# Phase tables made whole in the setup, and sums of MLP weight factors made during the mixer blocks

## The chip, the cores and the metric

One core of one Trainium2 chip runs the whole program. The metric is the device time of one execution in microseconds; lower is better.

## What is computed

One layer of a hybrid encoder over 2048 positions (16 learned meta tokens are put ahead and dropped at the end), width 1024. A chunked SSD mixer (16 heads of 64, state 128, short causal convolution) and an S5 mixer (32 groups of 16 channels, 64 complex states each) run side by side on the normed input, are gated and projected; a squared-ReLU MLP of width 4096 follows. All of it is held to float32 accuracy.

```
z, xbc, dt_raw, u_s5, gates = split(rmsnorm(h) @ w_in)
y_a = ssd_branch(z, xbc, dt_raw, ...)
y_b = s5_branch(u_s5, ...)          # h_t = a * h_(t-1) + B u_t, complex, causal
h = h + (sigmoid(g_a) * y_a + sigmoid(g_b) * y_b) @ w_out
h = h + square(relu(rmsnorm(h) @ w_ff_in)) @ w_ff_out
return rmsnorm(h)[:, 16:]
```

## The kernel before

Every large product is done as three: each operand is split into a rounded high part (`fp32r`, a cast on ScalarE) and the low rest (a subtraction on VectorE or GpSimd), and `mm3` (L243 to L245) issues high x high, high x low and low x high into one PSUM bank.

**Setup.** `s5_setup` is a generator that is pumped between the products of `u` (tiles `uw`, four blocks of 512 rows). It makes the S5 constants: powers of the discrete poles, the input and output matrices (`cst`), the causal kernels (`kpad`), and a table `tab` of phases, cosine and sine of k times eight steps' angle for 16 pairs of groups. `double` lengthens such a table by multiplying what is there by its last entry: six VectorE instructions per step. The table is made to `K0` = 64 entries and stored in the DRAM tile `tabd`. The recurrence needs KA + 1 = 259 entries.

**Mixer blocks.** Four blocks of 512 rows. In each, for four head groups: the convolved products (XBC), then the gate products (ZG), with the SSD steps hung behind them; then two more gate products (GB), the GLU products and the output products (OUT). Weights come in units of 0.5 MB that are split into 1 MB (`wu`, three buffers, two units fetched ahead). In block 0 the raw unit is loaded by SP (`wst`), split by ScalarE and GpSimd and stored (`wsd`); later blocks load the split unit through GpSimd's queue. In block 0 the whole S5 recurrence runs too, one of 16 pairs every two steps: `load_w` (L519) loads the pair's constants and the first 65 entries of its table into `s5tb` and lengthens them there to 259, in three steps of four VectorE instructions (L538 to L541) with the scratch tile `s5tu`. `states` uses the table, cosine and sine, in the lines L584, L585, L593 and L594.

**MLP.** Rows in three blocks of 768, 768 and 512, each cut in two halves; both products use Winograd's form of Strassen's scheme, seven products where eight would be, so that seven weight factors per group are wanted: three pieces of the weights themselves and four sums of them. There are 8 inner rounds (`di`) with four groups each, 28 products per round, 32 groups in all. In the first row block `Weights.make` loads two raw units per group through SP, makes the four sums on GpSimd (L1366 to L1369, L1380 to L1383), and for each factor `weight` casts (ScalarE, L1341), splits (VectorE or GpSimd by the table `ENG`, L1342) and stores it (SP, L1343) in the DRAM tile `wcd`. The factor's tile `wc` has three buffers, and one factor is made ahead of the product that is running. The other two row blocks read the factors back through GpSimd's queue (L1352).

**What sets the order.** Each engine works its instructions off in order. The order is made by a scheduler from the order in which the program is written; `tc.issue_after(mm)` holds back only those instructions that stand on the engine of `mm`. Loads and stores on SP, and GpSimd's loads, stand in the order of those engines.

```
            tu = pl.tile([P, P], F32, name="s5tu", tag="s5tu")
            done = K0
            while done < KA:
                ...
                V.scalar_tensor_tensor(tb[:, 1, o_], xi, yr, tu[:, :m], op0=ALU.mult, op1=ALU.add)
```

## Time and profile before

| | us |
|---|---|
| median of 3 runs | 3317.12 (3313.74 to 3323.17) |
| the profiled execution's own time | 3315.93 |
| its span, first to last instruction | 3314.2 |

| engine | busy us | share of the span | instructions |
|---|---|---|---|
| TensorE | 3087.5 | 93% | 18353 |
| VectorE | 2119.2 | 64% | 4364 |
| ScalarE | 1227.8 | 37% | 2569 |
| GpSimd | 1417.8 | 43% | 1736 |

The profile is one execution; the times of its stages are read from stretches of it, given in us from the span's start. A row of a stretch gives each engine's busy time, the share of TensorE's clock that was granted, the mean busy share of the 16 transfer engines, and what they moved. Matmuls are pipelined, so that TensorE's busy time is an upper bound of its work. A wait is put down to the event that came last. The shares over the whole span say little, since the stages have different limits.

### The profile page before, as it was taken

The numbers are of one execution on the slowest core, as the hardware profiler recorded it, in microseconds if no ns is written. First come the engines' busy times: TensorE is split into PE (matmuls) and PEld (weight loads), VectorE is DVE, ScalarE is ACT, GpSimd is POOL, SyncE is SP. The second block draws the span as 40 slices with busy tenths as digits, with TensorE's granted clock in tenths as the row PEclk, the third lists the DMA queues.
The fourth block names the chain that finished last, engine by engine and source line by source line (L and its number), as shares of the span: only waits on it lengthen the run. The fifth ranks groups of instructions, "written<-read, shape, count | busy, mean of one in ns | idle before, by whom it ended". The sixth has DMA issues, their size and how long they took to land. (4 is left out here: it accounts for less than half of the span.)

```text
span 3314.2 us, 50076 instructions
## 1 busy us (share of the span) xinstructions
PE 3087.5 (93%) x18353; PEld 2747.0 (83%) x18353; DVE 2119.2 (64%) x4364; ACT 1227.8 (37%) x2569; POOL 1417.8 (43%) x1736
## 2 busy tenths in 40 slices
PE   7989889998999999998999889898979999989998
PEld 6678777887888778876788788888879999989998
DVE  8689999526844476426764577667675555475555
ACT  5354444434422443324433443334442121142222
POOL 3356566523522244213442465665652222243343
PEclk9999989999999999999999999999999999999999
DMA  6376665775555654565756767777788888889998
GB/s 225 117 220 172 186 168 170 280 248 185 171 197 187 220 156 168 204 229 179 226 174 210 275 254 268 261 272 267 268 292 282 248 248 247 247 286 369 360 358 279
DMA packets 299493, 776.56 MB, mean 234 GB/s; under 512 B 94736, under 2 KB 136848, under 8 KB 270448
## 3 DMA queue, kind: packets, MB, share of 16 engines
q0 software_dynamic: 88832, 411.21, 37.3%
q1 hardware_dynamic: 207808, 360.93, 33.0%
q8 instruction: 146, 2.39, 0.3%
q10 hardware_dynamic: 2608, 1.22, 0.1%
q14 instruction: 99, 0.81, 0.1%
HBM read 560.48 MB, written 214.88 MB: 234 GB/s over the span
## 5 line engine op out<-in xcount | busy, mean ns | idle before, releaser
L1501 DVE TENSOR_TENSOR acc<-acc,p 128x512 f32<-128x512 f32 x330 | 225.8, 684 | 167.0 <-PE p L245 164.8
L243 PE MATMUL pd<-hnh,wc 128*128 128x384 f32 (+1 forms) x896 | 291.2, 326 | 30.9 <-DMA wc<-wcd 20.6
L243 PE MATMUL pd<-wu,xnh 128*128 128x512 f32 x768 | 310.9, 405 | 4.0 <-DMA wu<-wsd 3.1
L245 PE MATMUL pd<-wu,xnl 128*128 128x512 f32 x768 | 310.5, 405 | 0.0
L244 PE MATMUL pd<-wu,xnh 128*128 128x512 f32 x768 | 309.5, 403 | 0.0
L245 PE MATMUL pd<-hnh,wc 128*128 128x384 f32 (+1 forms) x896 | 290.0, 327 | 14.2 <-DVE wc L1342 11.7
L244 PE MATMUL pd<-hnl,wc 128*128 128x384 f32 (+1 forms) x896 | 290.1, 324 | 0.0
L227 POOL DMA_DIRECT2D wu<-wsd x168 | 96.0, 572 | 374.2 <-PE pd L245 309.0
L243 PE MATMUL pd<-xnh,wu 128*128 128x512 f32 (+1 forms) x640 | 232.1, 363 | 9.0 <-DMA wu<-wsd 8.9
L1352 POOL DMA_DIRECT2D wr<-wcd x227 | 121.1, 534 | 273.7 <-PE pd L245 135.0
L244 PE MATMUL pd<-xnl,wu 128*128 128x512 f32 (+1 forms) x640 | 230.2, 360 | 0.0
L245 PE MATMUL pd<-xnh,wu 128*128 128x512 f32 (+1 forms) x640 | 229.9, 360 | 0.0
L1352 POOL DMA_DIRECT2D wc<-wcd x221 | 117.4, 531 | 254.5 <-PE pd L245 136.6
L243 PEld LDWEIGHTS pd<-hnh,wc 128*128 128x128 f32 x896 | 172.1, 192 | 36.4 <-ACT hnh L990 12.2
L749 DVE SCALAR_TENSOR_TENSOR cacc<-craw,conv,cacc 128x512 f32<-128x512 f32 (+1 forms) x192 | 172.1, 897 | 31.8 <-ACT cacc L746 27.1
L245 PEld LDWEIGHTS pd<-hnh,wc 128*128 128x128 f32 x896 | 172.1, 192 | 20.8 <-DVE wc L1342 15.0
L217 POOL TENSOR_TENSOR wu<-wst,wu 128x1024 fp32r<-128x1024 f32 x56 | 137.6, 2458 | 90.7 <-ACT wu L216 85.6
L243 PEld LDWEIGHTS pd<-wu,xnh 128*128 128x128 f32 x768 | 146.8, 191 | 34.9 <-DMA wu<-wsd 4.0
L245 PEld LDWEIGHTS pd<-wu,xnl 128*128 128x128 f32 x768 | 147.2, 192 | 31.6
L244 PEld LDWEIGHTS pd<-wu,xnh 128*128 128x128 f32 x768 | 147.1, 191 | 31.0 <-issue 0.2
L244 PEld LDWEIGHTS pd<-hnl,wc 128*128 128x128 f32 x896 | 172.2, 192 | 0.0
L243 PEld LDWEIGHTS pd<-xnh,wu 128*128 128x128 f32 x640 | 125.2, 196 | 26.1 <-issue 10.8
(1012 smaller groups left out, 9984.0 us busy)
## 6 DMA issues: line engine op xcount, KB each, us to landing
wu<-wsd POOLq DMA_DIRECT2D x168, 1024.0 KB, 5.2
wr<-wcd POOLq DMA_DIRECT2D x227, 512.0 KB, 5.0
wcd<-wc SPq DMA_DIRECT2D x224, 512.0 KB
wc<-wcd POOLq DMA_DIRECT2D x221, 512.0 KB, 5.5
wsd<-wu SPq DMA_DIRECT2D x56, 1024.0 KB
wst<-in_w SPq DMA_DIRECT2D x60, 512.0 KB
csb<-csd SPq DMA_DIRECT2D x16, 1024.0 KB
xt<-in_x SPq DMA_DIRECT2D x28, 512.0 KB
```

The lines of the kernel that those rows point to most:

```text
L217: eng.tensor_tensor(t[:, 1], raw, t[:, 0].bitcast(F32), op=ALU.subtract)
L227: nc.gpsimd.dma_start(t, wsd[u - U_XBC])
L243: T.matmul(ps, lh, rh, start=first, stop=False, skip_group_check=open_)
L244: T.matmul(ps, lh, rl, start=False, stop=False, skip_group_check=open_)
L245: return T.matmul(ps, ll, rh, start=False, stop=last, skip_group_check=open_).ins
L749: V.scalar_tensor_tensor(acc[:, :n], raw[:, k:k + n], conv[:, mt, k:k + 1], acc[:, :n], op0=ALU.mult, op1=ALU.add)
L1352: nc.gpsimd.dma_start(t, wcd[di * 28 + j])
L1501: V.tensor_tensor(o, o, pv, op=ALU.add)
```

## The change

**Tables.** `K0` falls from 64 to 8: the setup makes 9 entries for all 16 pairs as before. A new function `phases` copies these for a quarter of the pairs (`NT` = 4) into a tile `tg`, lengthens them with `double` to 259 entries, six steps of six VectorE instructions, and stores them in `tabd`; it is called four times, after every second of the eight pieces of the setup. `load_w` loads the finished table, and its twelve VectorE instructions per pair are gone.

**Sums.** 30 of the 32 groups of MLP weights get their four sums early: 8 groups in mixer block 0, 9 in block 1, 9 in block 2, 4 in block 3 (`EARLY`). `ff_early` loads a group's two raw units through SP (tiles `era`, `erb`, two buffers), makes each sum (on VectorE in block 0, on GpSimd in the others), and `ff_split` casts it (ScalarE), splits it (VectorE) and stores it in `wcd` (SP). `early_step` draws these steps behind the units of the GLU and OUT products (in block 3 behind GLU alone). In the first MLP row block, the factors of these groups that are sums are loaded from `wcd` through GpSimd's queue into the same three `wc` buffers; the three plain pieces are made as before, with every split on VectorE. In all, 120 factors are made in the mixer blocks instead of the first row block and read back there once more.

```diff
-K0 = 64
+K0 = 8
+NT = 4
+EARLY = (8, 9, 9, 4)
...
-        nc.sync.dma_start(tabd, tab)
...
+        def phases(q0):
+            qs = slice(q0, q0 + NT)
+            tg = pl.tile([P, NT, 2, KA + 1], F32, name="tg", tag="tg")
+            S.copy(tg[:, :, :, 0:K0 + 1], tab[:, qs])
+            xa, xb = [x.rearrange("p q m -> p (q m)").rearrange("p (q m) -> p q m", q=NT) for x in (ua, ub)]
+            done = K0
+            while done < KA:
+                m = min(done, KA - done)
+                double(tg[:, :, 0, :], tg[:, :, 1, :], xa, xb, done, m)
+                done += m
+            nc.sync.dma_start(tabd[:, qs], tg)
...
+            if i % 2 == 1:
+                phases((i // 2) * NT)
...
-            nc.sync.dma_start(tb[:, :, 0:K0 + 1], tabd[:, q])
+            nc.sync.dma_start(tb, tabd[:, q])
...
-            tu = pl.tile([P, P], F32, name="s5tu", tag="s5tu")
-            done = K0
-            while done < KA:
...
-                V.tensor_scalar(tu[:, :m], xi, yi, None, op0=ALU.mult)
-                V.scalar_tensor_tensor(tb[:, 0, o_], xr, yr, tu[:, :m], op0=ALU.mult, op1=ALU.subtract)
-                V.tensor_scalar(tu[:, :m], xr, yi, None, op0=ALU.mult)
-                V.scalar_tensor_tensor(tb[:, 1, o_], xi, yr, tu[:, :m], op0=ALU.mult, op1=ALU.add)
-                done += m
...
+    def ff_sums(g, v, room, eng):
+        a11, a12, a21, a22 = v
...
+        if g % 4 < 2:
+            s1 = tt("s1", a21, a22, ALU.add)
+            yield 4, s1
+            s2 = tt("s2", s1, a11, ALU.subtract)
+            yield 1, s2
+            yield 2, tt("s3", a11, a21, ALU.subtract)
+            yield 6, tt("s4", a12, s2, ALU.subtract)
...
+    def ff_split(t, w, eng, i):
+        S.copy(t[:, 0], w)
+        eng.tensor_tensor(t[:, 1], w, t[:, 0].bitcast(F32), op=ALU.subtract)
+        nc.sync.dma_start(wcd[i], t.rearrange("p a k n -> p (a k n)").bitcast(F32))
+
+    def ff_early(pl, groups, eng):
+        def load(g):
+            wa, wb = [pl.tile([P, D], F32, name=nm, tag="er", bufs=2) for nm in ("era", "erb")]
+            ff_load(g, wa, wb)
+            return wa, wb
+        raw = load(groups[0])
+        for n, g in enumerate(groups):
+            v, m = ff_pieces(g, *raw)
...
+            for j, w in ff_sums(g, v, room, eng):
+                t = pl.tile([P, 2, m, 512 // m], F32R, name="ew", tag="ew", bufs=2)
+                ff_split(t, w, V, g * 7 + j)
+                if j == (6 if m == 4 else 3) and n + 1 < len(groups):
+                    raw = load(groups[n + 1])
+                yield
...
+        early = ff_early(pool("early%d" % b, stack=e_st, side="right"), range(g0, g0 + EARLY[b]), G if b else V)
+        slots = 8 if b == NB - 1 else 16
...
-            rhs_group([(b, U_GLU + q * 2 + i) for i in range(2)], y5h, y5l, evac_glu)
+            rhs_group([(b, U_GLU + q * 2 + i) for i in range(2)], y5h, y5l, evac_glu, step=early_step)
...
         def make(self):
...
+            for g in range(32):
+                wa, wb = ff_raw(fw, "wa"), ff_raw(fw, "wb")
+                ff_load(g, wa, wb)
...
+                ws = {0: a11, 3: a12, 5: a22} if m == 4 else {0: a11, 2: a21, 6: a22}
+                early = g < sum(EARLY)
+                if not early:
+                    ws |= dict(ff_sums(g, v, lambda nm: ff_sum(fw, nm).rearrange("p (k n) -> p k n", k=m), G))
+                for j in range(7):
+                    if j in ws:
+                        yield self.weight(ws[j], "v" if early else ENG[g % 4][j], m, g * 7 + j)
+                        continue
+                    t = wcs[0].tile([P, D], F32R, name="wc", tag="wc", bufs=wcs[1])
+                    nc.gpsimd.dma_start(t, wcd[g * 7 + j])
+                    yield t.rearrange("p (a k n) -> p a k n", a=2, k=m)
```

The order on three engines shows it. On VectorE in mixer block 0, before the change, the steps of a pair's table (`s5tu`, `s5tb`) stand among the convolution (`cacc`) and the SSD output (`y`):

```order
L538 TENSOR_SCALAR s5tu<-s5tb 128x64
L749 SCALAR_TENSOR_TENSOR cacc<-craw,conv,cacc 128x528
L870 TENSOR_SCALAR yss<-yss 128x1
L860 TENSOR_TENSOR y__3611<-y__3611,py 128x256
L539 SCALAR_TENSOR_TENSOR s5tb<-s5tb,s5tu 128x64
L860 TENSOR_TENSOR y__3611<-y__3611,py 128x256
L540 TENSOR_SCALAR s5tu<-s5tb 128x64
L866 TENSOR_TENSOR y__3611<-y__3611,zg 128x256
L541 SCALAR_TENSOR_TENSOR s5tb<-s5tb,s5tu 128x64
```

With the change that engine's table work stands in the setup, here the step of 128 entries of one quarter, among the low parts of the normed rows (`xnl`) that the `u` products wait for:

```order
L361 TENSOR_TENSOR ua<-tg 128x512
L362 TENSOR_TENSOR ub<-tg 128x512
L279 SCALAR_TENSOR_TENSOR xnl<-ntp,wmix,xnh 128x128 x2
L363 TENSOR_TENSOR tg<-ua,ub 128x4x128
L279 SCALAR_TENSOR_TENSOR xnl<-ntp,wmix,xnh 128x128 x2
L364 TENSOR_TENSOR ua<-tg 128x512
L365 TENSOR_TENSOR ub<-tg 128x512
L279 SCALAR_TENSOR_TENSOR xnl<-ntp,wmix,xnh 128x128
L366 TENSOR_TENSOR tg<-ua,ub 128x4x128
```

The table work has left the stretch where pairs and SSD steps alternate, for the one where the normed rows are made. On SP in the last products of mixer block 0, with the change:

```order
L227 DMA wsd<-wu 128x2048
L217 DMA wst<-in_w 128x1024
L938 DMA wcd<-ew 128x1024 x2
L908 DMA era<-in_w 128x1024
L1308 DMA yt<-yd 128x512
L938 DMA wcd<-ew 128x1024
L909 DMA erb<-in_w 128x1024
L938 DMA wcd<-ew 128x1024 x2
```

Loads and stores of the early sums (`era`, `erb`, `wcd<-ew`) stand between the unit loads (`wst`) and the last load of S5 outputs (`yt`), where before `wsd` and `wst` alternated alone. On GpSimd in the first MLP row block, before the change:

```order
L1380 TENSOR_TENSOR t_20651<-w2b,w2a 128x512
L1381 TENSOR_TENSOR t_20652<-w2a 128x512
L1382 TENSOR_TENSOR t_20653<-w2b,t_20652 128x512
L1342 TENSOR_TENSOR wc<-w1a,wc 128x512
L1342 TENSOR_TENSOR wc<-s_20491,wc 128x512
L1342 TENSOR_TENSOR wc<-w1b,wc 128x512
L1383 TENSOR_TENSOR t_20654<-w2b,t_20653 128x512
```

and with the change, over more than one inner round:

```order
L1457 DMA wc<-wcd 128x1024 x13
L1492 TENSOR_TENSOR fs2l<-ks_20306,fs2h 128x384
L1457 DMA wc<-wcd 128x1024 x3
L1492 TENSOR_TENSOR fs2l<-ks_20305,fs2h 128x384
L1457 DMA wc<-wcd 128x1024 x13
```

Sums and splits of weights are replaced there by loads; the splits `fs2l` of the MLP's inner activations remain.

## Rows read from the trace of the kernel before

**Rows 1.** Stretches by stage: start:end and length, busy us, clock, DMA share, GB/s.
```profile
0.00:155.00 155.00, 131.92 (x682) 100.08 (x683) 124.95 (x434) 80.44 (x206) 58.79 (x74) 0.98 0.54 174
155.00:605.00 450.00, 409.51 (x2407) 348.71 (x2406) 398.54 (x877) 210.91 (x454) 259.68 (x260) 0.94 0.64 191
...
706.00:1086.00 380.00, 367.66 (x1773) 301.49 (x1772) 207.15 (x492) 140.46 (x297) 127.36 (x202) 0.99 0.56 190
...
1864.00:2450.00 586.00, 521.16 (x3396) 499.52 (x3395) 407.78 (x566) 233.92 (x431) 356.74 (x260) 0.97 0.75 271
2461.00:2952.00 491.00, 484.38 (x3381) 480.86 (x3382) 286.70 (x481) 117.35 (x235) 144.57 (x241) 0.99 0.82 252
2952.00:3314.00 362.00, 330.17 (x2666) 326.54 (x2664) 203.26 (x423) 94.09 (x243) 143.31 (x246) 0.96 1.01 343
```
Busy times stand in the order TensorE's matmuls, its weight loads, VectorE, ScalarE, GpSimd, each with its count.

**Rows 2.** VectorE's lines, 155 to 605 us: count, busy us, mean ns, idle before.
```profile
L538 DVE TENSOR_SCALAR s5tu<-s5tb 128x64 f32<-128x64 f32 (+2 forms) x48 | 26.5, 551 | 1.7 <-DMA s5tb<-tabd 1.4
L539 DVE SCALAR_TENSOR_TENSOR s5tb<-s5tb,s5tu 128x64 f32<-128x64 f32 (+2 forms) x48 | 25.0, 521 | 0.4
L540 DVE TENSOR_SCALAR s5tu<-s5tb 128x64 f32<-128x64 f32 (+2 forms) x48 | 23.2, 484 | 0.4
L541 DVE SCALAR_TENSOR_TENSOR s5tb<-s5tb,s5tu 128x64 f32<-128x64 f32 (+2 forms) x48 | 21.7, 452 | 0.2
...
L595 DVE TENSOR_TENSOR s5t<-s5t,s5t 128x258 f32<-128x258 f32 x16 | 14.4, 900 | 0.2
...
L587 DVE TENSOR_TENSOR s5t<-s5t,s5t 128x258 f32<-128x258 f32 x16 | 7.9, 491 | 0.0
```

**Rows 3.** The tile `s5tb`, one of its lines: minimum, median and maximum in ns.
```profile
L538 DVE TENSOR_SCALAR s5tu<-s5tb x48: 208/286/2459, 174.5 to 534.8; 128x64 f32<-128x64 f32 x16, 128x128 f32<-128x128 f32 x16, 128x2 f32<-128x2 f32 x16
```

**Rows 4.** VectorE's lines by form, 40 to 80 us: table steps of the setup.
```profile
L360 DVE TENSOR_TENSOR tab<-ua,ub 128x512 f32<-128x512 f32 x1 | 0.7, 683 | 0.0
...
L360 DVE TENSOR_TENSOR tab<-ua,ub 128x128 f32<-128x128 f32 x1 | 0.3, 277 | 0.0
...
L363 DVE TENSOR_TENSOR tab<-ua,ub 128x32 f32<-128x32 f32 x1 | 0.2, 185 | 0.0
```

**Rows 5.** A stretch of dense products of 512 columns, columns as in rows 1.
```profile
706.00:730.00 24.00, 24.00 (x108) 19.43 (x107) 8.03 (x19) 10.18 (x17) 6.00 (x14) 1.00 0.82 272
```

**Rows 6.** Stretches from the last GB product to the end of blocks 0, 1; GLU on, block 3.
```profile
580.00:706.00 126.00, 125.33 (x591) 101.03 (x590) 48.51 (x97) 51.45 (x103) 56.91 (x37) 1.00 0.80 287
961.00:1086.00 125.00, 125.00 (x592) 101.20 (x591) 42.59 (x97) 34.39 (x84) 23.26 (x37) 1.00 0.63 219
...
1754.00:1864.00 110.00, 101.82 (x471) 82.66 (x470) 55.99 (x85) 37.60 (x74) 44.11 (x47) 0.97 0.64 220
```

**Rows 7.** Stretches of six inner rounds of the first MLP row block, five of the second.
```profile
1943.20:2372.70 429.50, 385.19 (x2523) 369.58 (x2523) 304.00 (x420) 169.40 (x313) 266.41 (x193) 0.97 0.74 267
2588.90:2888.00 299.10, 298.37 (x2102) 297.32 (x2101) 163.98 (x280) 60.53 (x120) 84.85 (x151) 1.00 0.82 247
```

**Rows 8.** ScalarE's waits, 1865 to 2450 us: total us, times, longest.
```profile
ACT wc L1341 <- DMA wcd<-wc: 156.8, 99, 6.4
```

**Rows 9.** Timelines of SP and of ScalarE, 2153 to 2161 us: start, length, instruction, idle before.
```profile
2155.05 5.76 SPq L1343 DMA_DIRECT2D wcd<-wc  x3
...
2159.87 0.62 ACT L1341 CAST wc<-w1a 128x512 fp32r<-128x512 f32 x1 [0.20 <-DMA wcd<-wc]
```

**Rows 10.** Issues of transfers, 2550 to 2900 and 2952 to 3314 us: KB, median us to landing.
```profile
wc<-wcd POOLq DMA_DIRECT2D x72, 512.0 KB, 4.6
...
wc<-wcd POOLq DMA_DIRECT2D x125, 512.0 KB, 5.9
```

**Rows 11.** Lines of GpSimd and VectorE, 1943 to 2300 us: splits of weight factors.
```profile
L1342 POOL TENSOR_TENSOR wc<-t,wc 128x512 fp32r<-128x512 f32 x20 | 28.5, 1426 | 1.9 <-ACT wc L1341 1.8
...
L1342 DVE TENSOR_TENSOR wc<-w1a,wc 128x512 fp32r<-128x512 f32 x10 | 6.9, 686 | 3.9 <-ACT wc L1341 3.9
```

**Rows 12.** The page, part 6: issues of the mixer blocks' split units.
```profile
wu<-wsd POOLq DMA_DIRECT2D x168, 1024.0 KB, 5.2
```

More of the change, by code (lines that the diff above doesn't have):

```diff
@@ L190, in _body @@
     kpad = dr.tile([16, SG, 256], F32, name="kpad")
-    tabd = dr.tile([P, NQ, 2, K0 + 1], F32, name="tabd")
+    tabd = dr.tile([P, NQ, 2, KA + 1], F32, name="tabd")
     h2d = dr.tile([SEQ, D], F32, name="h2d")
@@ L354, in double @@
             xr, xi = re[:, :, 1:1 + m], im[:, :, 1:1 + m]
-            yr = re[:, :, done:done + 1].broadcast_to([P, NQ, m])
-            yi = im[:, :, done:done + 1].broadcast_to([P, NQ, m])
+            nq = re.shape[1]
+            yr = re[:, :, done:done + 1].broadcast_to([P, nq, m])
+            yi = im[:, :, done:done + 1].broadcast_to([P, nq, m])
             a_, b_, o_ = ta[:, :, :m], tb[:, :, :m], slice(1 + done, 1 + done + m)
@@ L363, in double @@
             V.tensor_tensor(im[:, :, o_], a_, b_, op=ALU.add)
-        ua = pl.tile([P, NQ, K0 // 2], F32, name="ua")
-        ub = pl.tile([P, NQ, K0 // 2], F32, name="ub")
+        ua = pl.tile([P, NQ, P * NT // NQ], F32, name="ua")
+        ub = pl.tile([P, NQ, P * NT // NQ], F32, name="ub")
         for m in (1, 2, 4):
@@ L887, in decays, with ff_pieces, ff_load @@
         return t
+    def ff_pieces(g, wa, wb):
+        if g % 4 < 2:
+            v = [x.rearrange("p (a k n) -> p a k n", a=2, k=4)[:, i] for x in (wa, wb) for i in range(2)]
+            return v, 4
+        v = [x.rearrange("p (k a n) -> p k a n", k=2, a=2)[:, :, i, :] for x in (wa, wb) for i in range(2)]
+        return v, 2
+    def ff_load(g, wa, wb):
+        di, j = divmod(g, 4)
+        ua, ub = (U_FFI + 4 * di + 2 * j, U_FFI + 4 * di + 2 * j + 1) if j < 2 else \
+            (U_FFO + 4 * di + j - 2, U_FFO + 4 * di + j)
+        nc.sync.dma_start(wa, d["w"][ua])
+        nc.sync.dma_start(wb, d["w"][ub])
@@ new lines, in ff_sums, with tt @@
+    def ff_sums(g, v, room, eng):
+        a11, a12, a21, a22 = v
+        def tt(nm, x, y, op):
+            o = room(nm)
+            eng.tensor_tensor(o, x, y, op=op)
+            return o
+        if g % 4 < 2:
+            s1 = tt("s1", a21, a22, ALU.add)
[4 more added lines that the diff above has]
+            yield 6, tt("s4", a12, s2, ALU.subtract)
+        else:
+            yield 1, tt("t3", a22, a12, ALU.subtract)
+            t1 = tt("t1", a12, a11, ALU.subtract)
+            yield 4, t1
+            t2 = tt("t2", a22, t1, ALU.subtract)
+            yield 5, t2
+            yield 3, tt("t4", a21, t2, ALU.subtract)
@@ new lines, in ff_split, with room @@
+    def ff_split(t, w, eng, i):
[10 more added lines that the diff above has]
+            v, m = ff_pieces(g, *raw)
+            def room(nm):
+                return pl.tile([P, 512], F32, name=nm, tag="es", bufs=3).rearrange("p (k n) -> p k n", k=m)
+            for j, w in ff_sums(g, v, room, eng):
[4 more added lines that the diff above has]
+                yield
@@ L1255, in _body, with early_step @@
         ml = gp.tile([P, 8, TB], F32R, name="mixl")
+        e_st = ExitStack()
+        g0 = sum(EARLY[:b])
+        early = ff_early(pool("early%d" % b, stack=e_st, side="right"), range(g0, g0 + EARLY[b]), G if b else V)
+        slots = 8 if b == NB - 1 else 16
+        early_n = [0, 0]
+        def early_step(mm):
+            early_n[0] += 1
+            want = -(-early_n[0] * EARLY[b] * 4 // slots)
+            with tc.issue_after(mm):
+                while early_n[1] < want:
+                    early_n[1] += 1
+                    next(early, None)
         for q in range(4):
@@ L1279, in _body @@
         if b == NB - 1:
+            for _ in early:
+                pass
+            e_st.close()
             y5_st.close()
@@ L1301, in evac_out @@
                 S.activation(jk, xr, AF.Square, accum_out=ssh[:, n, i:i + 1])
-            rhs_group([(b, U_OUT + n * 4 + i) for i in range(4)], mh, ml, evac_out)
+            rhs_group([(b, U_OUT + n * 4 + i) for i in range(4)], mh, ml, evac_out, step=early_step if b < NB - 1 else None)
         if b < NB - 1:
@@ L1306, in _body @@
             row_scale(ssh[:, 0, b * NC4:(b + 1) * NC4], rsh[:, b * NC4:(b + 1) * NC4], NC4)
+        for _ in early:
+            pass
+        e_st.close()
         g_st.close()
@@ L1340, in weight @@
             t = wcs[0].tile([P, 2, n, 512 // n], F32R, name="wc", tag="wc", bufs=wcs[1])
-            S.copy(t[:, 0], w)
-            (V if eng == "v" else G).tensor_tensor(t[:, 1], w, t[:, 0].bitcast(F32), op=ALU.subtract)
-            nc.sync.dma_start(wcd[i], t.rearrange("p a k n -> p (a k n)").bitcast(F32))
+            ff_split(t, w, V if eng == "v" else G, i)
             return t
@@ new lines, in make @@
+            for g in range(32):
+                wa, wb = ff_raw(fw, "wa"), ff_raw(fw, "wb")
+                ff_load(g, wa, wb)
+                v, m = ff_pieces(g, wa, wb)
+                a11, a12, a21, a22 = v
+                ws = {0: a11, 3: a12, 5: a22} if m == 4 else {0: a11, 2: a21, 6: a22}
[9 more added lines that the diff above has]
+                    yield t.rearrange("p (a k n) -> p a k n", a=2, k=m)
```

34 lines of the change are left out of this document (removed).

## The prediction

> **What bounds the kernel now.** I read the stages first, then the stretch of each stage that the change touches. Row by row, the stages [rows 1] show three pictures. In the setup (0 to 155 us) and the first mixer block with its S5 recurrence (155 to 605 us) VectorE is the busiest engine: 125.0 of 155 us and 398.5 of 450 us, and TensorE runs at 0.94 of its clock in the block, with holes. In the next block (706 to 1086) VectorE falls to 207 of 380 us and TensorE is nearly solid. In the MLP's first row block (1864 to 2450) TensorE has 521 of 586 us, while the second, with the same products (3396 and 3381 records), takes 491 us at 484 busy. So 95 us hang on how the first block gets its weights, and some part of 450 us on VectorE's work in block 0. The reader is to see that these are the two places of the change, and that it pays in two others: the setup, and the last products of each mixer block, where TensorE is solid [rows 6].
>
> **Part one, the phase tables.** Removed from block 0: 192 instructions on `s5tu` and `s5tb`, busy 26.5 + 25.0 + 23.2 + 21.7 = 96.4 us [rows 2]. They last 0.45 to 0.55 us on average, with a median near 0.3 [rows 3], so 192 x 0.3 = 57 us is their own work and some 39 us is waiting, most likely for GpSimd: the adds of L595 take 900 ns beside its work, those of L587 with the same shape 491 [rows 2].
>
> What this gives is bounded by TensorE. 24.0 us hold 108 products of 512 columns in a dense stretch [rows 5], 0.222 us each. Block 0's 450 us hold 576 of these (128 us), 768 of 264 columns (by columns 0.115, I take 0.125: 96 us), and 2407 - 1344 = 1063 smaller ones (an estimate of 0.12: 128 us), in sum 352 us. The next block priced alike is 1344 x 0.222 + 429 x 0.12 = 350 of 380 us, 0.92. At 0.92 block 0 would need 383 us, 67 less; VectorE at its present share would need (398.5 - 57) / 0.886 = 385 us, or less. I take -50, since the S5 chain hands each pair from TensorE to VectorE, ScalarE and GpSimd and back, which the next block does not have; the ends are -30 (half of the 57) and -80.
>
> Added to the setup: four quarters of 36 instructions. By form, one lasts 185 ns at 32 elements (and at 8, I take it), 277 at 128 and 683 at 512 [rows 4], between these some 212 at 64 and 415 at 256: 6 x 1.96 x 4 = 47 us. Removed there are the three largest steps over all 16 pairs, 6 x (0.277 + 0.415 + 0.683) = 8 us. Net 39 us on an engine that is idle for 30 of the setup's 155 us. If four fifths of this idle time take work, 39 - 24 = 15 us are left on the path. Ends: 0 (starts of neighbours overlap by some 80 ns, and the tables of later quarters are not wanted at once) and 39. Four copies on ScalarE, three more stores on SP, and table loads of 265 KB in place of 65 lie beside 0.54 and 0.64 of DMA use [rows 1]: nothing.
>
> **Part two, the MLP's weight factors.** In the first row block each product's factor lives in a ring of three buffers. Six of eight inner rounds take 429.5 us for 168 products [rows 7], 2.557 us each, so a buffer turns in 7.67 us. In one turn [rows 9] the store is issued at 2155.05, and the next cast into that buffer, released by the store, stands at 2159.87: 4.8 us are the store. Over the stage 99 casts wait 156.8 us for a store [rows 8]. The ring, not an engine's load, sets the pace; a product alone takes 299.1 / 140 = 2.136 us [rows 7].
>
> After the change three of seven factors are still made and stored, and four are loaded. A made turn loses GpSimd's sums and its splits of 1.4 us; VectorE's split lasts 0.7 us [rows 11], and with the cast's 0.62 [rows 9] and an allowance of 0.7 for queues a turn is 0.62 + 0.7 + 0.7 + 4.8 = 6.8 us. A loaded turn is 0.2 us of hand-over (the gap in [rows 9]) + load + 2.136. The load is 4.6 us in the second row block, at 247 GB/s [rows 7, 10], and 5.9 in the third at 343 GB/s [rows 1, 10]. The stage moves 271 x 0.586 = 159 MB now and as much afterwards, as 63 MB of stores become loads; over some 550 us that is 288 GB/s, which lies two fifths of the way: 5.1 us. Loaded turn 7.4, mean (3 x 6.8 + 4 x 7.4) / 7 = 7.2 us, 2.39 a product, 224 x (2.557 - 2.39) = -37 us. Ends: -4 with loads of 5.9 us, -94 at 2.136. GpSimd's 120 issues of loads replace as many sums and about as many splits, and cost the path nothing while it is idle; they stand in order around its splits of `fs2l`, two per round, which wait for ScalarE. That is left to the ends.
>
> Moved into the mixer blocks' last products: per group two loads and four stores of 0.524 MB, 3.15 MB; four sums, four casts, four splits. Engine work is covered: block 0 gets 64 VectorE instructions of 0.69 us, 44 us over 48.5 of 126; the next blocks 36 sums of some 1.4 us on GpSimd, 50 us over 23 of 125 [rows 6, 11]. The cover is thin for the queues. SP issues in order, and block 0's raw unit loads now stand behind stores that wait for a split; from block 1 on GpSimd's unit loads stand behind sums that wait for their raw loads. Two units are fetched ahead, 2 x 24 x 0.222 = 10.7 us, and such a load lands in 5.2 us [rows 12], so 5 us of delay are free. Block 0: 126 x 287 GB/s = 36 MB and 8 x 3.15 = 25 MB are 61 MB in 126 us; blocks 1 and 2: 27 + 28 = 56 MB in 125 us; block 3: 24 + 13 in 110. A mean of 343 GB/s over a long stretch is the highest seen [rows 1]. At that the extra time is 53, 37, 37 and 0 us. The other end is nothing: the transfers run on under the next block (190 GB/s over all, [rows 1]), since nothing waits for the stores but the room that the next block takes. I take +14, +5, +5 and +3, nearer to the low end, as 0.2 to 0.4 of these stretches' DMA time is idle [rows 6].
>
> On transfers the Trainium skill has a rule that speaks against this part (DMA: Bandwidth & Descriptors, Specifications): about 358 GB/s of HBM traffic per core. By it block 0's 61 MB would take 170 us and cost 44 us rather than 14. No stretch of over 100 us here exceeds it.
>
> **Sum** against the profiled execution (3315.9 us, span 3314.2): +15 - 50 + 27 - 37 = -45, 3271 us; the median of the runs is 1.2 us higher, so **3272 us**.
>
> **Rivals.**
> - *Transfers bind in the last products* (slower). Place: SP's queue in block 0 and the shared transfer engines in blocks 0 to 2. Price: the full +127 us in place of 27, so +55: 3372. It decides from tails of some 70 us on. For it: 0.80 DMA use in block 0 already [rows 6]. Against: idle transfer time, and the stores' late end. The skill's rule of 358 GB/s, above, gives most of it.
> - *The ring stays the bound*: loads take 5.9 us, -4 for -37: 3305. For it: the third row block. Against: there far more buffers ask at once.
> - *The table work only moves*: setup +39, block 0 -30, the rest -10: 3316, no change. For it: the waits on GpSimd, which the remaining instructions inherit. The Trainium skill says that a VectorE instruction with two SBUF inputs and a GpSimd one that reads SBUF shut each other out (SBUF — State Buffer, Who interferes with whom); the 900 against 491 ns agree. The new multiplies are of this kind, and the setup's GpSimd multiplies stand beside them.
> - *Everything is covered*: the first row block reaches 2.136 us (-94) and the tails cost 5: 15 - 50 - 94 + 5 = -124, 3193.
>
> **How the numbers follow.** A measurement of this kernel tells about 0.3%, 10 us, from no change. Chances: forecast 0.53, everything covered 0.17, ring 0.13, moved only 0.07, transfers 0.10. Faster: 0.52 + 0.17 + two thirds of the ring's + little = 0.79. Same: the rest of the ring's, half of "moved only" and a bit, 0.08. Slower: 0.13. The range runs from 3200, half-way into the covered case, to 3318; the transfer case and the far end of the covered one are left out.
>
> **What would show it.** Right: no `s5tu` in block 0, its 450 us near 400 with VectorE under 0.85; U products that end some 15 us later; inner rounds of the first row block near 67 us in place of 71.6, with ScalarE's wait for stores well down; the 125 us from the second gate product to the end of block 1 no longer than 130. Wrong: `wc` loads above 5.5 us there; TensorE waiting for units or for `xr` in the last products; VectorE still at 0.9 in block 0.

## The result, and the profile after

The changed kernel takes 3447.8 us (median of 4 runs, 3445.1 to 3455.1) against 3316.9 us before: 1.039 times as long, with a 95% interval of 1.037 to 1.041. The forecast was 3272 us, faster. The profiled execution took 3448.7 us, with a span of 3447.0.

The stages of after, columns as in [rows 1]; in order the setup, block 0's groups, its last products, block 1's last products, block 2's groups and last products, block 3's last products, and the eight inner rounds of the MLP's first row block.

```profile
0.00:163.90 163.90, 133.83 (x680) 101.30 (x680) 146.07 (x542) 82.04 (x209) 63.31 (x74) 0.93 0.54 178
163.90:592.80 428.90, 395.87 (x2408) 340.47 (x2407) 361.85 (x708) 212.82 (x456) 265.18 (x260) 0.97 0.71 210
592.80:727.60 134.80, 110.59 (x473) 86.26 (x471) 86.39 (x135) 55.43 (x113) 52.29 (x34) 0.91 0.96 365
...
1018.60:1140.00 121.40, 106.69 (x472) 83.27 (x470) 61.02 (x109) 41.77 (x100) 58.32 (x60) 0.96 0.92 332
1140.00:1433.20 293.20, 272.53 (x1301) 223.37 (x1302) 177.54 (x419) 120.44 (x235) 117.17 (x178) 0.97 0.59 202
1433.20:1561.70 128.50, 107.90 (x471) 84.90 (x470) 62.61 (x111) 42.92 (x102) 59.84 (x60) 0.93 0.94 337
...
1863.10:1978.90 115.80, 102.92 (x469) 82.69 (x469) 66.94 (x98) 44.10 (x88) 49.65 (x53) 0.96 0.84 293
1978.90:2564.10 585.20, 504.96 (x3273) 478.86 (x3272) 324.75 (x536) 160.17 (x303) 104.55 (x151) 0.98 0.81 260
```

Read it against [rows 1] and [rows 6]. The last products, where TensorE was solid, now have holes (110.6 of 134.8 us busy in block 0), a granted clock of 0.91 to 0.96, and transfers at 0.92 to 0.96 of their time in blocks 0 to 2 (0.84 in block 3). In the first row block GpSimd is busy 105 us in place of some 357 [rows 1], and the block is no shorter.

The same boundaries (the first matmul of a stage) read from every kernel's trace give the table on which the rest of this text rests; "last" are a block's GLU and OUT products together, "MLP 1" the eight inner rounds of the first row block, all in us. The names are those of the experiments below. The median is that of all runs; the stages are those of one profiled execution and add up to its span.

| kernel | median | setup | b0 | last 0 | b1 | last 1 | b2 | last 2 | b3 | last 3 | MLP 1 | rest |
|---|---|---|---|---|---|---|---|---|---|---|---|---|
| before | 3316.9 | 154.6 | 450.3 | 101.4 | 279.8 | 99.7 | 275.6 | 100.0 | 293.0 | 109.3 | 567.5 | 882.9 |
| after | 3447.8 | 163.9 | 428.9 | 134.8 | 291.0 | 121.3 | 293.2 | 128.5 | 301.4 | 115.8 | 585.1 | 882.9 |
| tables | 3305.0 | 164.2 | 426.6 | 101.5 | 280.2 | 99.7 | 276.6 | 100.1 | 293.7 | 108.4 | 565.2 | 886.1 |
| early | 3449.1 | 153.9 | 449.4 | 137.7 | 291.2 | 123.8 | 289.1 | 125.9 | 300.2 | 117.8 | 576.2 | 882.5 |
| dead | 3433.0 | 165.9 | 427.2 | 135.9 | 289.4 | 123.4 | 288.2 | 127.7 | 301.3 | 115.4 | 568.0 | 886.0 |
| dead16 | 3391.1 | 162.8 | 427.8 | 131.7 | 280.4 | 121.4 | 280.3 | 126.1 | 292.3 | 112.1 | 563.7 | 884.8 |
| dead16_pre | 3373.8 | 164.5 | 427.6 | 123.8 | 285.6 | 108.8 | 281.8 | 118.2 | 298.5 | 108.8 | 564.2 | 886.2 |
| nowork | 3328.9 | 163.8 | 427.0 | 109.9 | 281.1 | 106.2 | 277.9 | 101.3 | 291.8 | 111.7 | 565.6 | 886.6 |
| nodma | 3363.2 | 165.3 | 428.8 | 125.9 | 283.7 | 119.2 | 277.5 | 116.8 | 290.4 | 109.6 | 560.0 | 887.2 |
| nodma_pipe | 3368.2 | 164.5 | 428.1 | 124.4 | 283.7 | 116.5 | 278.9 | 117.4 | 292.2 | 112.7 | 563.1 | 886.2 |
| nodma_nosum | 3325.7 | 163.8 | 427.1 | 110.7 | 279.9 | 105.1 | 276.6 | 104.6 | 295.7 | 106.5 | 560.9 | 885.9 |
| nodma_sumonly | 3333.9 | 163.9 | 429.7 | 111.1 | 279.9 | 103.1 | 277.9 | 103.2 | 304.4 | 115.3 | 563.7 | 884.1 |
| after_r4 | 3380.0 | 163.9 | 429.6 | 135.6 | 290.8 | 127.6 | 292.9 | 126.5 | 299.8 | 109.6 | 526.6 | 878.7 |
| tables_r4 | 3316.3 | 164.8 | 427.4 | 101.4 | 280.2 | 99.7 | 275.5 | 100.9 | 291.0 | 111.8 | 579.8 | 879.2 |
| before_r4 | 3328.4 | 154.2 | 451.9 | 101.4 | 278.1 | 99.9 | 276.9 | 100.0 | 295.6 | 110.5 | 581.3 | 882.1 |
| tables_r4s3 | 3281.2 | 164.4 | 426.6 | 101.4 | 280.0 | 99.7 | 276.0 | 99.9 | 294.2 | 107.8 | 541.0 | 884.7 |
| before_tab2 | 3382.1 | 154.5 | 513.5 | 100.7 | 277.8 | 99.7 | 279.2 | 99.9 | 289.5 | 110.0 | 575.2 | 882.2 |
| tables_less | 3296.6 | 165.7 | 422.0 | 101.4 | 280.6 | 99.7 | 275.4 | 99.9 | 293.2 | 111.3 | 562.5 | 885.7 |

In the changed kernel the four last products took 90.0 us more (33.4 + 21.6 + 28.5 + 6.5), the three blocks behind them 37.2 more, the first row block 17.6 more, the setup 9.3 more and block 0's groups 21.4 less: +132.7, the whole difference of the spans.

TensorE's waits and the landing of units in block 1's last products (1018.6 to 1140 us; engine, line, what it waited for: total us, times, longest) show one end of it: units that landed in 5.2 us [rows 12] take 8.6.

```profile
PE pd L245 <- DMA wu<-wsd: 9.1, 4, 4.5
```

```profile
wu<-wsd POOLq DMA_DIRECT2D x16, 1024.0 KB, 8.6
```

In block 0 the longest wait is for the S5 rows `yt`, whose loads land 9.8 and 7.7 us after their issue:

```profile
PE y5p L1312 <- ACT yt L1309: 10.0, 2, 5.4
```

In the four stretches of last products together TensorE's busy time is 428.1 of 500.5 us, with the tables alone (`tables`, below) 401.3 of 409.6: 64 us more of standing still, and 27 us more for the same products at a lower granted clock. Of 68 us of waits there, 47 are for loads that land late (`yt`, units, the residual rows `xr`) and 2 for VectorE's evacuations of the gate (`gth`).

### The profile page after: what moved, and what is told of

Same layout as the page of the kernel before. It is cut to its first block, busy times and chain, and to the rows that moved or that the text cites. A ratio compares the mean times of both kernels' runs of the same rounds, so it can differ in the third digit from the quotient of the medians.

```text
span 3447.0 us, 50518 instructions
## 1 busy us (share of the span) xinstructions
PE 3121.6 (91%) x18353; PEld 2759.1 (80%) x18353; DVE 2157.6 (63%) x4435; ACT 1225.5 (36%) x2572; POOL 1302.5 (38%) x1719
## 5 line engine op out<-in xcount | busy, mean ns | idle before, releaser
L245 PE MATMUL pd<-wu,xnh 128*128 128x512 f32 x768 | 316.8, 413 | 21.6 <-DMA wu<-wsd 16.9
L246 PE MATMUL pd<-wu,xnh 128*128 128x512 f32 x768 | 313.5, 408 | 0.0
L247 PE MATMUL pd<-hnh,wc 128*128 128x384 f32 (+1 forms) x896 | 289.5, 325 | 0.1
L1457 POOL DMA_DIRECT2D wc<-wcd x120 | 64.1, 534 | 442.9 <-PE pd L247 190.4
L1439 POOL DMA_DIRECT2D wc<-wcd x221 | 118.3, 536 | 254.0 <-PE pd L247 134.9
L754 DVE SCALAR_TENSOR_TENSOR cacc<-craw,conv,cacc 128x512 f32<-128x512 f32 (+1 forms) x192 | 179.2, 935 | 12.4 <-ACT cacc L751 9.5
```

Source lines behind the costliest of these rows:

```text
L245: T.matmul(ps, lh, rh, start=first, stop=False, skip_group_check=open_)
L246: T.matmul(ps, lh, rl, start=False, stop=False, skip_group_check=open_)
L247: return T.matmul(ps, ll, rh, start=False, stop=last, skip_group_check=open_).ins
L754: V.scalar_tensor_tensor(acc[:, :n], raw[:, k:k + n], conv[:, mt, k:k + 1], acc[:, :n], op0=ALU.mult, op1=ALU.add)
L1439: nc.gpsimd.dma_start(t, wcd[di * 28 + j])
L1457: nc.gpsimd.dma_start(t, wcd[g * 7 + j])
```

## The experiments

**The two parts apart (tables, early).** `tables` sets `EARLY` to zeros, `early` keeps the old table code.

```diff
-EARLY = (8, 9, 9, 4)
+EARLY = (0, 0, 0, 0)
```

> The tables alone, no early sums; the MLP makes all its factors as in the kernel before. If the stage times of the changed kernel belong to the parts that stand in them: U products and first part of the setup +9, block 0's groups -21, all else as before, so 3317 + 9 - 21 = 3305 us (3298 to 3312). Rival, the prediction's own size: the early sums' transfers had taken from block 0's gain, and alone it gives -50 with a setup of +9 to +15, 3276 to 3282 us. Second rival: the later stages of the changed kernel are slow because block 0 ends in another order, then this one is slow too, above 3330 us.

Measured 3305.0 us, 0.996 of before (0.994 to 0.998): as the stages said.

> The early sums alone, the tables as in the kernel before. If the parts add: 3448 + 12 = 3460 us (3450 to 3470), with the last products of the blocks at about +29, +22, +29, +7 us, the starts of the next blocks at +11, +18, +8, and the MLP's first row block at +17. If the tables were part of the loss in the tails, less than 3448 us.

Measured 3449.1 us, 11 less than the sum of the parts. The tables alone gain 12 us, the early sums lose 132; beside the sums the tables' gain is 1 us. By the stages what is lost of it stands in MLP 1 (585.1 us with the tables, 576.2 without); why, no run shows.

**The early work without its readers (dead), and with few bytes stored (dead16).** The MLP makes everything itself; the early factors go to a scratch `wce`.

```diff
-                early = g < sum(EARLY)
+                early = False
...
-                ff_split(t, w, V, g * 7 + j)
+                ff_split(t, w, V, g * 7 + j, wce)            # dead
+                ff_split(t, w, V, g * 7 + j, wce, D // 16)   # dead16
```

> As the changed kernel, but the MLP makes all of its factors itself, and the early sums go to a scratch of their own that nobody reads. The theory that the loss lies in two places, the last products with the next blocks' starts (+124 us) and the MLP's first row block with its loaded factors (+17): row block 1 back at about 597 us, the tails as slow as in the changed kernel, 3448 - 17 = 3431 us (3424 to 3438). Rival: the first row block is slow because the stage before leaves it something (clock, late stores), not because of its loads: 3448 us, row block 1 at 614.

Measured 3433.0 us, MLP 1 at 568.0: the loaded factors themselves cost the first row block 15 to 17 us (in `early`, one profile, 9).

> As the run with the unread early sums, but of each early factor only a sixteenth is stored (64 of 1024 elements per partition): the same instructions, waits and queue order, 35 in place of 94 MB. Transfers bind: the tails and the next blocks' starts lose most of their 124 us, for what idle transfer time covers comes first; 3322 to 3350 us. Rival, the order of the queue (SP stands behind the splits, GpSimd's unit loads behind the sums) or the engines' work: no change against the run with whole stores, about 3431 us.

Measured 3391.1 us, between the two. The stores' bytes cost 42 us, and 26 of these stand in the next blocks' starts: b1, b2 and b3 fall by 9.0, 7.9 and 9.0, all of it within the first 200 of the 960 matmuls that each has with units. The last products stay slow at this load of the transfers, block 1's GLU and OUT:

```profile
1002.70:1065.30 62.60, 55.39 (x257) 43.79 (x255) 48.02 (x88) 29.11 (x73) 37.45 (x38) 0.95 0.61 209
1065.30:1124.10 58.80, 50.71 (x217) 39.13 (x216) 27.08 (x28) 17.08 (x34) 28.14 (x27) 0.97 0.78 269
```

So there the stores' bytes are not the main cause, which was my theory so far.

**Loads without work (nowork), work without loads and stores (nodma).**

```diff
-            for j, w in ff_sums(g, v, room, eng):
...
-                ff_split(t, w, V, g * 7 + j)
+            for j in ((4, 1, 2, 6) if m == 4 else (1, 4, 5, 3)):                          # nowork
+                nc.sync.dma_start(wce[g * 7 + j][:, :D // 16], raw[0][:, :D // 16])
...
             for j, w in ff_sums(g, v, room, eng):                                         # nodma
                 t = pl.tile([P, 2, m, 512 // m], F32R, name="ew", tag="ew", bufs=2)
-                ff_split(t, w, V, g * 7 + j)
-                if j == (6 if m == 4 else 3) and n + 1 < len(groups):
-                    raw = load(groups[n + 1])
+                S.copy(t[:, 0], w)
+                V.tensor_tensor(t[:, 1], w, t[:, 0].bitcast(F32), op=ALU.subtract)
```

> As the run with sixteenth stores (3391 us), without the early sums, casts and splits: the raw loads and as many small stores stay in SP's order. Left out: the early sums, which nobody read. There the gate and output products cost 81 us more than with the tables alone (30, 22, 26, 4 us in blocks 0 to 3) at 0.6 to 0.8 of DMA time. Theory now: ScalarE, VectorE and GpSimd take their work in order, and a cast that waits for sums that wait for a raw load holds up the evacuations behind it; then the tails come back to within 5 us each and the time is 3305 to 3320 us. Rival: SP's order and the raw loads' traffic alone hold up TensorE's units and rows: above 3370 us.

Measured 3328.9 us, 24 over `tables`, a little above the theory's range: SP's order, the raw loads and the small stores do cost something.

> As the run with sixteenth stores, but one raw load per block, whose tiles serve all of its groups, and no early stores: sums, casts and splits stay, their waits for loads and stores go. Left out: the other groups' values, which nobody read. If the waits for raw loads are the cost, blocks 1 and 2 come back to within 5 us (GLU and OUT some 51 and 49 us) and block 0, where VectorE has both sums and splits, to within 12: 3310 to 3330 us. If the work itself is the cost (VectorE and GpSimd in each other's way, ScalarE's casts ahead of evacuations), the tails stay: 3370 us and more.

Measured 3363.2 us, between the two ranges: the engine work alone costs 58 us, mostly in GLU (77.6, 69.6 and 63.4 us in place of 53.0, 51.3 and 51.3), where it bunches: of the 30 splits in block 1's last products 27 stand there. So the waits for loads are not all of it. 24 + 58 = 82 is nearly the 86 of `dead16`, but by total alone: over the cost with `tables`, GLU of blocks 0 to 2 is 47 us longer in `dead16` and 67 in the two runs added, OUT 31 and 10. With the loads, part of the work moves on into OUT (18 and 16 splits in `dead16`); in the changed kernel 14 of the 27 splits in block 1's last products stand in GLU. How much the engine work costs beside whole stores, no run shows.

**Raw loads one group earlier (dead16_pre), work staggered (nodma_pipe).** The first looks two groups ahead (k = 2, in block 0 k = 1); the second emits, at each step, the next sum, the split before and this cast.

```diff
-            wa, wb = [pl.tile([P, D], F32, name=nm, tag="er", bufs=2) for nm in ("era", "erb")]
+            wa, wb = [pl.tile([P, D], F32, name=nm, tag="er", bufs=2 * k) for nm in ("era", "erb")]
...
-                    raw = load(groups[n + 1])
+                    raws.append(load(groups[n + k]))
...
+            nxt = next(todo, None)                                                        # nodma_pipe
+            if t:
+                V.tensor_tensor(t[0][:, 1], t[1], t[0][:, 0].bitcast(F32), op=ALU.subtract)
...
+                S.copy(t[0][:, 0], w[1])
+            w = nxt
```

> As the run with sixteenth stores, with each group's raw loads issued one group earlier in blocks 1 to 3 (four raw tiles in place of two, two sum tiles in place of three, one scratch tile for the squares). If the raw loads' landing inside a group is what stalls the engines, blocks 1 and 2 fall from +22 and +26 us to under +10 each, 3350 to 3365 us. If the engines' own work is the cost, 3385 to 3395 us.

Measured 3373.8 us, 17 less, half-way: the loads' landing inside a group is part of it.

> As the run whose early work has one raw load per block and no stores (3363 us, gate products 77.6, 69.6, 63.4 us in blocks 0 to 2), with the same sums, casts and splits staggered: at each step the sum of the step after, the cast of this one, the split of the one before, so that no engine waits at its place in the order for another's work of the same step. If those in-order waits are the 58 us, the gate products fall to 55 to 60 us and the time to 3315 to 3330 us. If the work itself is the cost (VectorE's adds and GpSimd's beside each other, the casts' time on ScalarE), 3350 us and more.

Measured 3368.2 us, no better. Waits of one engine for another's work of the same step are not the 58 us; the work is.

**Which work (nodma_nosum, nodma_sumonly).** From `nodma`, either the sums or the casts and splits are left out.

```diff
-            for j, w in ff_sums(g, v, room, eng):
+            for j, w in ((j, next(vs)) for j in range(4)):    # nodma_nosum; vs: the raw pieces in turn
...
             for j, w in ff_sums(g, v, room, eng):             # nodma_sumonly
-                S.copy(t[:, 0], w)
-                V.tensor_tensor(t[:, 1], w, t[:, 0].bitcast(F32), op=ALU.subtract)
                 yield
```

> As the run whose early work has one raw load per block and no stores (3363 us), without the sums: casts and splits are made of the raw pieces. Left out: the early sums, which nobody read. If VectorE and GpSimd beside each other are the cost, VectorE has 0.69 us a split again, and blocks 1 and 2's gate products fall from 69.6 and 63.4 us to within 4 us of 51.3: 3310 to 3325 us. If the splits in VectorE's order are the cost, blocks 1 and 2 keep more than half of their 18 and 12 us, and the time stays above 3340 us.

> The same with the sums and without casts and splits. Left out: the early factors' halves, which nobody read. If the two engines beside each other are the cost, GpSimd's sums stretch only the few gate multiplies, and blocks 1 and 2's gate products stay within 5 us of 51.3: 3305 to 3320 us (block 0, where VectorE makes the sums, the same). If GpSimd's sums alone are the cost (the gate's last add stands behind them on GpSimd), blocks 1 and 2 stay above 60 us and the time above 3335.

Measured 3325.7 and 3333.9 us: 21 and 29 us over `tables`, the first just at the end of the first theory's range, the second 14 above it, against 58 together. Of the 29, by the profile, 18 stand in block 3, 11 of them in its groups (b3), well ahead of any of this work; what that is, no run shows. In the last products of blocks 1 and 2 `nodma` is 36.2 us over `tables`, the splits alone 9.9, the sums alone 6.5: some 20 us are there only when both are. VectorE's lines in block 1's GLU (count, busy us, mean ns, idle before), of `tables`, `nodma`, `nodma_nosum` and `nodma_sumonly`:

```profile
L1347 DVE SCALAR_TENSOR_TENSOR gth<-sgb,gth 128x256 f32<-128x256 f32 x15 | 7.4, 495 | 0.4
L1345 DVE SCALAR_TENSOR_TENSOR gth<-gth,pd 128x256 f32<-128x256 f32 x15 | 6.3, 420 | 17.0 <-ACT gth L1344 16.9
```

```profile
L956 DVE TENSOR_TENSOR ew<-t,ew 128x512 fp32r<-128x512 f32 x16 | 20.2, 1271 | 0.3
L956 DVE TENSOR_TENSOR ew<-s,ew 128x512 fp32r<-128x512 f32 x12 | 15.0, 1246 | 0.5 <-ACT ew L955 0.2
L1347 DVE SCALAR_TENSOR_TENSOR gth<-sgb,gth 128x256 f32<-128x256 f32 x14 | 11.9, 846 | 0.2
...
L1345 DVE SCALAR_TENSOR_TENSOR gth<-gth,pd 128x256 f32<-128x256 f32 x14 | 5.7, 410 | 3.5 <-ACT gth L1344 3.5
```

```profile
L957 DVE TENSOR_TENSOR ew<-erb,ew 128x512 fp32r<-128x512 f32 x12 | 8.5, 725 | 0.7 <-ACT ew L956 0.6
L1348 DVE SCALAR_TENSOR_TENSOR gth<-sgb,gth 128x256 f32<-128x256 f32 x15 | 7.0, 467 | 0.2
L957 DVE TENSOR_TENSOR ew<-era,ew 128x512 fp32r<-128x512 f32 x10 | 6.8, 699 | 2.5 <-ACT ew L956 2.5
```

```profile
L1344 DVE SCALAR_TENSOR_TENSOR gth<-sgb,gth 128x256 f32<-128x256 f32 x14 | 13.9, 992 | 0.4
```

A split takes 0.70 to 0.73 us without GpSimd's sums and 1.25 to 1.27 beside them; the gate multiply of two SBUF tiles 0.47 to 0.50 and 0.85 to 0.99. The multiply `gth<-gth,pd`, which reads one of its two from PSUM, takes 0.41 to 0.42 in all four. The Trainium skill has this rule (SBUF — State Buffer, Who interferes with whom): a VectorE instruction with two SBUF inputs and a GpSimd instruction that reads SBUF exclude each other. These rows agree. VectorE has 27.4 of 50.9 us in that stage with the tables, and with the early work 62.7 of 69.3: it has become the busiest engine, and the gate's evacuations stand in its queue: of TensorE's 12.0 us of idle time there 9.3 are waits for one.

```profile
PE pd L246 <- DVE gth L1345: 9.3, 2, 5.6
```

In block 0, where VectorE makes the sums too and GpSimd splits the units, VectorE is busy 74.0 of GLU's 77.5 us. Block 1's GLU in `tables`, `nodma` and `nodma_nosum`:

```profile
972.50:1023.40 50.90, 50.90 (x249) 41.66 (x248) 27.40 (x69) 19.68 (x54) 14.67 (x22) 1.00 0.50 174
```

```profile
1003.70:1073.00 69.30, 57.34 (x252) 45.86 (x251) 62.65 (x96) 33.70 (x82) 54.21 (x49) 0.90 0.38 129
```

```profile
981.50:1037.50 56.00, 51.75 (x253) 41.96 (x252) 39.93 (x92) 30.30 (x77) 15.76 (x22) 1.00 0.47 160
```

**Block 0 (before_tab2, tables_less).** The table work twice over in the kernel before; and, in `tables`, the four sums and differences of `states` left out.

```diff
-            while done < KA:
+            for done in (64, 128, 256, 64, 128, 256):                                     # before_tab2
...
-            V.tensor_tensor(t1[:, 0, :], t1[:, 0, :], t2[:, 0, :], op=ALU.add)            # tables_less
-            V.tensor_tensor(t1[:, 1, :], t1[:, 1, :], t2[:, 1, :], op=ALU.subtract)
...
-            V.tensor_tensor(t1[:, 0, :], t1[:, 0, :], t2[:, 0, :], op=ALU.subtract)
-            V.tensor_tensor(t1[:, 1, :], t1[:, 1, :], t2[:, 1, :], op=ALU.add)
```

> The kernel before, whose block 0 makes each phase table twice over (192 more instructions, the same values), to read block 0's price of this work from the other side. If VectorE sets block 0's pace throughout, the block grows by the 57 us of own work that the rows give: 3374 us. If the block takes 0.4 of it, as the removal did (24 of 57 us), 3341 us (3332 to 3350). If waits for GpSimd come with the work and are lost with it, the whole 96 us: 3413 us.

> The tables alone, with four more VectorE instructions per pair left out of block 0's S5 states: the sums and differences of the rotated terms, before and after the scan (64 instructions, 8.5 + 8.7 + 13.4 + 14.8 = 45 us by their rows). If VectorE still sets the block's pace, it falls by 45 us, to 3260 us. If the chain or TensorE has become the bound, by 10 us or less, 3295 to 3305. At the 0.4 that the tables' removal gave, 18 us: 3287 us.

Measured 3382.1 us (+65) and 3296.6 us (-8). Block 0 of `before_tab2`, `tables` and `tables_less`:

```profile
154.50:668.00 513.50, 432.08 (x2408) 367.35 (x2407) 458.95 (x1070) 212.37 (x454) 260.29 (x260) 0.88 0.57 167
```

```profile
164.20:590.80 426.60, 396.75 (x2408) 341.91 (x2407) 357.41 (x703) 211.99 (x454) 267.25 (x260) 0.96 0.72 211
```

```profile
165.70:587.70 422.00, 393.81 (x2409) 336.56 (x2408) 324.98 (x639) 211.62 (x454) 261.72 (x260) 0.98 0.73 214
```

Above the kernel before, VectorE sets the pace to the full (+63 us of block for +60 of busy time); below it, 24 us are to be had for the first 42 of busy time, the tables, and 5 for the next 32. VectorE falls from 0.84 to 0.77 of the block, TensorE stands at 0.93 in both: VectorE is no longer the bound. Whether TensorE's own products or the hand-overs between the engines are, no run separates.

**The ring (after_r4, tables_r4, before_r4, tables_r4a2, tables_r4s3, tables_r4s3a2).** A fourth `wc` buffer in place of the fourth raw tile; a2 asks for two factors ahead.

```diff
-NRAW = 4
+NRAW = 3
-    wcs = [fw, 3]
+    wcs = [fw, 4]
```

> The changed kernel with a ring of four factor buffers in the first row block, and three raw tiles in place of four (the same memory). Theory: the ring's turn of 0.2 + 5.0 us of landing + 2.1 us of product, over three buffers, sets the pace there; over four it is 1.8 us a product, below TensorE's own 2.14, and the first row block goes from 614 us to some 505 (500 to 520), the time to 3448 - 109 = 3339 us (3330 to 3355). Rival: traffic, GpSimd's queue or the clock sets the pace of the loads: 600 us and more, 3430 to 3448 us.

Measured 3380.0 us, 68 less; six inner rounds of 64.5 us on average in place of 72.6. The ring is the bound of the changed kernel's first row block, though less than I priced. TensorE's waits for factors there, of after and of `after_r4`:

```profile
PE pd L245 <- DMA wc<-wcd: 30.4, 24, 5.4
PE p L245 <- DMA wc<-wcd: 22.3, 28, 2.5
```

```profile
PE pd L245 <- DMA wc<-wcd: 8.5, 7, 3.9
PE p L245 <- DMA wc<-wcd: 4.3, 6, 1.4
```

> The tables alone, with a ring of four factor buffers in the MLP's first row block and three raw tiles in place of four. If the stores' turn of 7.7 us over three buffers sets the pace there, four make 1.9 us a product, under TensorE's 2.14: inner rounds near 62 us in place of 70, the stage 65 to 75 us shorter, 3305 - 70 + 7 (the last row block's start, as the run with four buffers showed) = 3242 us (3230 to 3255). Rival: with three raw tiles the raw loads come late and hold up GpSimd's sums, inner rounds of 68 us and more, above 3285 us.

> The kernel before with the ring of four factor buffers and three raw tiles, nothing else. By the same theory 3317 - 63 = 3254 us (3242 to 3267), and 12 us above the tables with the same ring if the two parts add. If the ring's gain is less here than with the tables, block 0's tables reach into the MLP, which no row so far shows.

Measured 3316.3 and 3328.4 us, 11 more than each without it: a miss. In six inner rounds ScalarE's wait for stores does go (101.7 us in `tables`, 20.1 in `tables_r4`), but TensorE now waits for VectorE's accumulations, 39.4 us where `tables` has 11.5 on this line. VectorE's instructions have become longer: 337.7 us for 420 of them, against 304.2 for 422. GpSimd's wait for raw loads, the rival's sign, is not new: with four raw tiles it is 50.7 + 18.0 us in `tables`. The two waits in `tables_r4`:

```profile
PE p L245 <- DVE acc L1574: 39.4, 12, 4.7
```

```profile
POOL s L917 <- DMA wb<-in_w: 47.3, 9, 7.2
```

> The tables alone with the ring of four, and factors asked for two products ahead in place of one. If in-order casts that stand behind the evacuation of the product before keep the fourth buffer from being used, inner rounds fall by another 1 to 3 us each, 3220 to 3235 us. Rival: the four buffers already cover the store, and asking earlier changes nothing, within 5 us of the run that asks one ahead; or the earlier cast stands ahead of an evacuation and delays it, up to 10 us more.

Measured 3318.9 us, as `tables_r4`.

`tables_r4s3` takes the room from the sums in place of the raw tiles: `NSUM = 3`, all four raw tiles, the fourth sum of a group made just before its use, and the first norm's temporaries put into `wc` tiles.

```diff
...
+                for n in range(3):
+                    k, x = next(sums)
+                    ws[k] = x
                 for j in range(7):
+                    if j == (6 if m == 4 else 3):
+                        k, x = next(sums)
+                        ws[k] = x
```

> The tables alone with a ring of four factor buffers in the MLP's first row block and all four raw tiles, the room taken from the sums (three tiles in place of five, each group's fourth sum made late). If with three raw tiles the late raw loads held up GpSimd's sums (51 us of its waits there), this one gives what the ring was to give: inner rounds of 60 to 64 us in place of 70, 3305 - 50 = 3255 us (3235 to 3275). If VectorE's splits, in its order ahead of the accumulations, set the pace of made factors, or the sums' scarcer tiles do, rounds of 69 us and more and 3300 to 3320 us.

Measured 3281.2 us, 0.988 of before (0.987 to 0.990): the version that beats both kernels. MLP 1 falls from 565.2 to 541.0 us, half of what I priced. TensorE's wait for accumulations is 16.2 us there, in six rounds, and GpSimd's for raw loads 5.6; the run does not separate the fourth raw tile from the later sum.

```profile
POOL s L917 <- DMA wb<-in_w: 5.6, 3, 5.0
```

> The tables with the ring of four and four raw tiles (3281 us), factors asked for two products ahead in place of one. If the chain of cast and split inside one product's time is what is left, rounds of 62 to 64 us in place of 67 and 3255 to 3270 us. If VectorE's full order or the raw loads are, no change, 3276 to 3288 us.

Measured 3281.6 us, no change; what holds the rounds at 67 us in place of 60 stays open.

## Why the prediction was wrong

Step by step, by its own terms.

- **Setup, +15:** measured +9.6 (`tables`). Right, and so is its term: VectorE's instructions on tables add up to 39.7 us more, forecast 39; the last quarter runs on into block 0.
- **Block 0, -50, ends -30 and -80:** measured -24, outside. The count of the work was right: all VectorE instructions of the block added up, 460.3 us before and 403.0 in `tables`, are 57.3 us fewer, so the other 39 us of the removed 96.4 now stand in other instructions. What failed is the step that let VectorE keep its share of 0.886, and the TensorE price of 352 us with it: VectorE has 0.84 of the block in `tables`, TensorE is busy 394 us even in `tables_less`, and the block stops following VectorE some 24 us down. The rival "the table work only moves" had the better size here.
- **Last products, +27, ends 0 and 127:** measured +126 with the starts behind them (after less `tables`: 90.7 + 35.1). Two steps failed. The first is "Engine work is covered": it compared sums of busy time over the whole 125 us, gave blocks 1 to 3 GpSimd's sums alone and left VectorE's splits there out, and so put engine work at nothing. By itself it costs 58 us (`nodma`): it bunches in GLU, sums and splits lengthen each other, VectorE's queue holds the evacuations.
- The second is the transfers' +27, which measured some 70. By the medians raw loads and SP's order cost 24 to 28 us (`nowork`; `dead16` less `nodma`) and the stores' bytes 42 (`dead` less `dead16`). The sentence that failed is "nothing waits for the stores but the room that the next block takes": 26 us of the 42 are in the next blocks' starts, and in block 2's GLU of the changed kernel ScalarE's casts of early factors wait 11.6 us for stores, with the casts of the next normed rows behind them in its order; TensorE waits 8.0 us for the low parts of those rows.
- How these divide in the changed kernel itself stays open: its own waits are mostly for late loads (47 of 68 us) and hardly for the gate's evacuations (2), the sum of the three parts is one of differences between runs, and loads and whole stores without engine work were not tried.
- **First row block, -37, ends -4 and -94:** measured +17 (after less `dead`, or less before). What I said would go did go: ScalarE's 156.8 us of waiting for stores [rows 8] are 18.2 us in the eight rounds. The step that failed is the mean turn of 7.2 us. Loads land in 4.7 us there, even below my 5.1, yet six inner rounds take 435.7 us for 168 products, 2.59 each and 7.8 a turn. A tenth of the loads take over 6.5 us, in a ring that is used in order, where an early one gives nothing back; how much of the turn that is was not tried. That three buffers are the bound, `after_r4` shows. TensorE waits 52.7 us for loaded factors and 10.5 for made ones. So the rival "the ring stays the bound" was right in kind, and still too cheap.

The sum was -45 and came out +133 between the profiled executions. The rival "transfers bind in the last products" had the price, 127 us, and I gave it 0.10. That its 127 meets the measured 126 is luck: by the medians transfers and SP's order are about half of it, and the other half is engine work that I had ruled out by an average. One reading was wrong as well: I wrote that no stretch of over 100 us exceeds 358 GB/s, but 2961 to 3111 us of the kernel before holds 370. Of my signs, TensorE waits for units and late `xr` in the last products came true, as "wrong" signs; `wc` loads above 5.5 us did not.

## What to carry to other kernels

Cover is to be read from the shortest stretch into which the new work falls, and from the queue in which it stands, not from busy time over the whole stage; and work of GpSimd beside work of VectorE is priced at the row in which the two stand side by side, here 1.26 us for a split of 0.70. A stage where TensorE is solid can pay for its holes twice, in time and in clock: here 64 and 27 us. Before factors are moved out of a stage, look at what the ring there waits for: a fourth buffer, with the raw tiles kept, took 24 us off the stage to which 120 factors made elsewhere added 17.

## What was not expected of the hardware

- In `nodma`, with 0.38 of the transfer time used, a GLU stage of 50.9 us grew to 69.3: TensorE's idle time explains 12.0 us of these 18.4, and 6.4 us are the same products at a mean granted clock of 0.90 in place of 1.00. TensorE had stood still for 5.6 and 3.7 us before 1030 and 1062 us; 1030 to 1035 and 1060 to 1065 us have a clock of 0.50 and 0.53, about the lower of its two levels of 1.2 and 2.4 GHz, where from 1003.7 to 1025 us it was 1.00.
- Block 0's last products moved 365 GB/s over 134.8 us, and the kernel before 370 over 150 us (2961 to 3111), where the highest mean of a whole stage was 343 [rows 1]. The Trainium skill gives about 358 GB/s of HBM traffic per core (DMA: Bandwidth & Descriptors, Specifications); all transfers of the core are in the two rows, and both are a little above that figure.
- A fourth factor buffer at the cost of a raw tile left the waits of ScalarE shorter and the stage 15 us longer, with the clock of six rounds at 0.91 against 0.97 (`tables_r4` against `tables`).
